# The experts' outputs added to the tokens two blocks at a time, the last squares summed on VectorE

## Chip, cores and metric

The kernel runs on one core of a Trainium2 chip. The metric is the device time of one execution in microseconds, the median of several runs.

## What is computed

A conformer convolution block with a feed-forward layer, then a second block: projections, a short convolution and a spatial gating unit, a mixture of 16 experts, and a last RMS norm. T = 256 tokens, D = 2048 features. Only the experts and the last norm matter here:

```python
def hierarchical_moe(x, w_rg, b_rg, w_re, b_re, w_gate, w_up, w_down):
    ...
    gate = ((pg * oh_g)[:, :, None] * w_inner[:, None, :]).reshape(-1, N_EXPERTS)
    hid = jax.nn.silu(jnp.einsum('td,edf->tef', t, w_gate)) * jnp.einsum('td,edf->tef', t, w_up)
    y = jnp.einsum('tef,efd->td', hid * gate[:, :, None], w_down)
    return y.reshape(bsz, s, d)

    ...
    h = h + hierarchical_moe(rms_norm_2(h, norm_ffn_g[l]), ...)
    return rms_norm_2(h, norm_final_g)
```

## The kernel before

Features lie on the 128 partitions: the tokens `h` are 16 blocks (KB) of 128 features by 256 tokens in float32. Weights are float32 in memory; each 128x1024 half of a weight tile is loaded by SyncE into one of 8 raw buffers, ScalarE makes a high part of it (`hi`, L75) and VectorE the rest (`lo`, L83). A raw buffer is loaded anew when its low part is done. TensorE multiplies by both parts, with separate records for loading the stationary operand (PEld) and for the product (PE).

In the experts' stage (`experts`, from about 1700 us) at most 64 tokens of each expert are gathered. For expert e, `into(e)` multiplies 16 halves of the gate and up weights into banks 0 and 1, `between(e)` makes the hidden values out of them (L1167 to L1200: copies out, two folds on TensorE, silu, product, high and low part), and `down(e)` multiplies 8 halves of the down weights; every two of these fill a bank, and ScalarE copies it to `Yt` (L1215). The turns run in 0, in 1, out 0, in 2, out 1 and so on. In the last turns (`out 13`, `out 14`, `in 15`) only the last expert's are different: out 13 and out 14 follow each other, and `out 15` ends the stage.

An expert's output is then put back at its tokens, a **scatter**: for block k a product of `Yt` with the placement matrix `scat[e]` into a bank of a ring of six, for two experts in one bank (the first and the last expert go alone), and an add of the bank to `h` by VectorE (L1152). The scatters wait in the list `todo`. After each half `fill` adds a credit of 0.5 us (0.3 in `into(15)`, 1 in `down(15)`, at most 1 in all) and takes scatters while the credit is above zero, each at 0.43 us times its experts. What has to follow on VectorE and ScalarE is put into `posts`, and `beat`, at the start of each half, writes all posts and then the next high and low parts. The stream is written ahead: at a half, the low part of the half two places later follows.

The order on each engine is the order in which the program writes it, and an engine that waits holds what is behind it. In the last expert's scatters an add is followed by a square on ScalarE (L1158, into `sq` with two buffers, into `acc` for blocks 0 and 8, into `lone` for the last three), and GpSimd adds the squares to `acc` (L535). `natural_sums` sums `acc` and the `lone`s on TensorE; the norm's factor and the 16 output blocks (L1278) follow.

Of the kernel before, what the change touches and what calls it, by code (L numbers as in the profile page):

```python
# [7 lines left out]
F32 = mybir.dt.float32  # L8
# [3 lines left out]
ACT = mybir.ActivationFunctionType  # L12
# [3 lines left out]
P = 128  # L16
D = 2048
KB = D // P
T = 256
# [111 lines left out]
def network(ctx, tc, a, out):  # L131
# [946 lines left out]
    def experts(hot, stream, extra):  # L1078
# [64 lines left out]
            scat[e], rsl[e] = sc, rs  # L1143

        def scatter(k, es):
            b, o = spare()
            for n, e in enumerate(es):
                mm(o[:, :T], Yt[e % 3][:, k * P : (k + 1) * P], scat[e], n == 0, n == len(es) - 1)
                left[e] -= 1

            def add():
                nc.vector.tensor_tensor(h[:, k, :], h[:, k, :], o[:, :T], OP.add)  # L1152
                if NE - 1 in es:
                    post(square)

            def square():
                sq = square_to(k)
                nc.scalar.activation(sq, h[:, k, :], ACT.Square)  # L1158
                post(lambda: add_square(sq, k, True))

            post(add, b)

# [39 lines left out]
        def down(e):  # L1202
            while e >= 3 and left[e - 3] > 0:
                todo.popleft()[1]()
            hd = hids.pop(e)
            left[e] = KB
            for c in range(4):
                b, o = taken()
                for n in range(2):
                    hi, lo = beat()  # L1210
                    for f in range(2):
                        product(o, hd[:, 2 * n + f, :], hi, lo, f, n == 0 and f == 0, n == 1 and f == 1)
                    if n == 1:
                        def out_of_bank(c=c, b=b, o=o):
                            nc.scalar.copy(Yt[e % 3][:, c * 512 : (c + 1) * 512], o)  # L1215
                            ring.append(b)

                            es = (e,) if e in (0, NE - 1) else (e - 1, e)
                            if e == NE - 1 or e % 2 == 0:
                                for k in range(4 * c, 4 * c + 4):  # L1220
                                    todo.append((0.43 * len(es), lambda k=k: scatter(k, es)))
                        post(out_of_bank)
                    fill(FILL_DOWN if e < NE - 1 else 1)

# [46 lines left out]
                posts.popleft()()  # L1271


        natural_sums(bank[2], 2, lone)
        rsqrt(rp, bank[2][:, :4:2], eps6)
        to_all(rp, bank[3][:, :T])
        for k in range(KB):
# [72 lines left out]
```

## Time and profile before

| what | value |
|---|---|
| median of 3 runs | 2271.34 us (2270.51 to 2272.91) |
| the profiled execution's own time | 2271.37 us |
| its span | 2269.6 us |
| PE busy, share of the span | 2217.8 us, 98% |
| PEld busy | 2077.4 us, 92% |
| DVE busy | 1597.0 us, 70% |
| ACT busy | 1256.9 us, 55% |
| POOL busy | 215.7 us, 10% |
| mean over the span, read and written | 224 GB/s |

PE is TensorE's products, PEld its loads of the stationary operand, DVE VectorE, ACT ScalarE, POOL GpSimd. Products are pipelined and their ends are modelled, so PE's 98% says little about how much room is left; where TensorE waits shows in the weight loads, whose rows carry the idle time ahead of them and what ended it. The stages differ, so shares are to be read by stage: the experts' stage lies between 1700 and 2254 us.

### The profile page before, as it was taken

What the parts mean: (1) busy time and instruction counts of PE and PEld (TensorE: products, weight loads), DVE (VectorE), ACT (ScalarE), POOL (GpSimd) and SP (SyncE); (2) the same over time, 40 slices, a digit from 0 to 9 for tenths busy, and PEclk for the clock granted to TensorE, in tenths of its full rate; (3) what the DMA queues carried; (4) which work ended last, traced back from release to release, by engine and by line L of the source; (5) the groups of instructions that cost most, each with busy time, mean ns of one, the idle gap of its engine ahead of it and who ended that gap; (6) DMA issues with size and microseconds to landing.
All of it is one profiled execution on the core that took longest, in us unless ns stands there. A gap on an engine that the chain in (4) does not pass through costs nothing. (4 is left out here: it accounts for less than half of the span.)

```text
span 2269.6 us, 41689 instructions
## 1 busy us (share of the span) xinstructions
PE 2217.8 (98%) x16539; PEld 2077.4 (92%) x16539; DVE 1597.0 (70%) x2259; ACT 1256.9 (55%) x1638; POOL 215.7 (10%) x162
## 2 busy tenths in 40 slices
PE   6999999999999999999999999999999999999996
PEld 6999899999999999999899999999977878778775
DVE  6999767655544455555875665566569899998996
ACT  4446554544434444444553444444578988878774
POOL 5798200000000000000100000000000000000001
PEclk8999999999999999999999999999999999999998
DMA  6554355565665566656656556656559999999993
GB/s 217 164 170 164 103 195 168 189 195 194 193 197 195 186 199 193 194 187 197 216 179 203 190 188 191 195 185 204 181 174 363 362 376 353 333 368 327 385 345 151
DMA packets 139964, 508.90 MB, mean 224 GB/s; under 512 B 15552, under 2 KB 15568, under 8 KB 139760
## 3 DMA queue, kind: packets, MB, share of 16 engines
q1 hardware_dynamic: 139104, 503.88, 65.2%
q8 instruction: 131, 2.15, 0.4%
q0 software_dynamic: 656, 2.27, 0.3%
q14 instruction: 73, 0.60, 0.1%
HBM read 503.99 MB, written 2.10 MB: 223 GB/s over the span
## 5 line engine op out<-in xcount | busy, mean ns | idle before, releaser
L83 DVE TENSOR_TENSOR lo<-raw,hi 128x1024 fp32r<-128x1024 f32 x884 | 1063.6, 1222 | 531.6 <-PE bank L164 468.0
L75 ACT CAST hi<-raw 128x1024 fp32r<-128x1024 f32 x952 | 987.0, 1054 | 738.9 <-PE bank L164 566.1
L164 PE MATMUL bank<-aH,hi 128*128 128x256 f32 (+1 forms) x3456 | 966.4, 280 | 6.3 <-ACT aH L243 4.7
L164 PE MATMUL bank<-aL,hi 128*128 128x256 f32 (+1 forms) x3456 | 960.2, 279 | 8.3 <-DVE aL L245 8.3
L164 PE MATMUL bank<-aH,lo 128*128 128x256 f32 (+1 forms) x3456 | 963.4, 279 | 0.0
L164 PEld LDWEIGHTS bank<-aH,hi 128*128 128x128 f32 x3456 | 653.2, 189 | 9.1 <-ACT aH L243 5.1
L164 PEld LDWEIGHTS bank<-aL,hi 128*128 128x128 f32 x3456 | 649.6, 189 | 9.8 <-DVE aL L245 9.5
L164 PEld LDWEIGHTS bank<-aH,lo 128*128 128x128 f32 x3456 | 653.0, 189 | 0.0
L535 POOL TENSOR_TENSOR acc<-acc,sq 128x256 f32<-128x256 f32 x23 | 18.5, 805 | 1913.8 <-ACT sq L676 723.4
L164 PE MATMUL bank<-hidH,lo 128*128 128x256 f32 x704 | 194.3, 276 | 0.0
L164 PE MATMUL bank<-hidH,hi 128*128 128x256 f32 x704 | 194.3, 276 | 0.0
L164 PE MATMUL bank<-hidL,hi 128*128 128x256 f32 x704 | 194.3, 276 | 0.0
L83 POOL TENSOR_TENSOR lo<-raw,hi 128x1024 fp32r<-128x1024 f32 x68 | 163.4, 2417 | 52.2 <-ACT hi L75 32.3
L284 DVE SCALAR_TENSOR_TENSOR bank<-glu,vec,bank 128x256 f32<-128x256 f32 x387 | 160.7, 482 | 1.9
L164 PEld LDWEIGHTS bank<-hidH,hi 128*128 128x128 f32 x704 | 132.2, 188 | 0.0
L164 PEld LDWEIGHTS bank<-hidL,hi 128*128 128x128 f32 x704 | 132.2, 188 | 0.0
L164 PEld LDWEIGHTS bank<-hidH,lo 128*128 128x128 f32 x704 | 132.2, 188 | 0.0
L164 PE MATMUL bank<-hi,aH 128*128 128x512 f32 x320 | 128.4, 418 | 0.8 <-ACT gu_first L1167 0.6
L164 PE MATMUL bank<-hi,aL 128*128 128x512 f32 x320 | 126.1, 410 | 0.0
L164 PE MATMUL bank<-lo,aH 128*128 128x512 f32 x320 | 122.8, 400 | 0.8 <-DVE lo L83 0.8
L164 PE MATMUL bank<-hi,hd_first 128*128 128x512 f32 x256 | 109.9, 429 | 0.7 <-DVE hd_first L1200 0.5
L164 PE MATMUL bank<-lo,aL 128*128 128x512 f32 x256 | 103.4, 404 | 0.6 <-DVE lo L83 0.6
(284 smaller groups left out, 2177.7 us busy)
## 6 DMA issues: line engine op xcount, KB each, us to landing
raw<-egu SPq DMA_DIRECT2D x256, 512.0 KB, 5.9
raw<-gu SPq DMA_DIRECT2D x176, 512.0 KB, 4.3
raw<-w SPq DMA_DIRECT2D x144, 512.0 KB, 4.3
raw<-edn SPq DMA_DIRECT2D x128, 512.0 KB, 6.1
raw<-dn SPq DMA_DIRECT2D x88, 512.0 KB, 4.3
raw<-cw_in SPq DMA_DIRECT2D x64, 512.0 KB, 3.6
raw<-cw_out SPq DMA_DIRECT2D x32, 512.0 KB, 3.9
raw<-wup SPq DMA_DIRECT2D x32, 512.0 KB, 4.5
```

Of the source, the lines that this page charges most:

```text
L75: self.nc.scalar.copy(hi, self.source(self.n_high))
L83: eng.tensor_tensor(lo, self.source(self.n_low), self.highs[self.n_low].bitcast(F32), OP.subtract)
L164: nc.tensor.matmul(o, l, r, start=start, stop=stop, skip_group_check=True)
L284: nc.vector.scalar_tensor_tensor(dw[:, j, :] if t == end - 1 else ta, gl, V("w_dw", j * TAPS + t), early[j % 2] if t == 1 else ta, OP.mult ...
L535: (nc.gpsimd if n or gpsimd else nc.vector).tensor_tensor(acc[:, n, :], acc[:, n, :], sq, OP.add)
```

## The change

`scatter(k, es)` now takes blocks k and k + 1: two products per expert into the two halves of one bank, and one add of 128x2x256 by VectorE. It is put on the list for every second block at twice the price, 0.86 us times its experts. In the last expert's scatters ScalarE squares both blocks in one instruction (into `acc` for blocks 0 and 1, into a buffer `sq2` of which there is one for the others, into two `lone`s for the last two), and VectorE, not GpSimd, adds the squares to the whole of `acc`. `natural_sums` takes two `lone`s instead of three.

```diff
--- before.py
+++ after.py
@@ -1143,20 +1143,31 @@
             scat[e], rsl[e] = sc, rs
 
         def scatter(k, es):
+
             b, o = spare()
-            for n, e in enumerate(es):
-                mm(o[:, :T], Yt[e % 3][:, k * P : (k + 1) * P], scat[e], n == 0, n == len(es) - 1)
-                left[e] -= 1
+            for i in range(2):
+                for n, e in enumerate(es):
+                    mm(o[:, i * T : (i + 1) * T], Yt[e % 3][:, (k + i) * P : (k + i + 1) * P], scat[e], i == 0 and n == 0, n == len(es) - 1)
+            for e in es:
+                left[e] -= 2
+            two = h[:, k : k + 2, :]
 
             def add():
-                nc.vector.tensor_tensor(h[:, k, :], h[:, k, :], o[:, :T], OP.add)
+                nc.vector.tensor_tensor(two, two, o.rearrange("p (i t) -> p i t", i=2), OP.add)
                 if NE - 1 in es:
                     post(square)
 
             def square():
-                sq = square_to(k)
-                nc.scalar.activation(sq, h[:, k, :], ACT.Square)
-                post(lambda: add_square(sq, k, True))
+                if k >= KB - 2:
+                    nc.scalar.activation(lone[0], two[:, 0], ACT.Square)
+                    nc.scalar.activation(lone[1], two[:, 1], ACT.Square)
+                    return
+                if k == 0:
+                    nc.scalar.activation(acc, two, ACT.Square)
+                    return
+                sq = tmp.tile([P, 2, T], F32, tag="sq2", bufs=1, name=f"last{k}_{turn_of[0]}")
+                nc.scalar.activation(sq, two, ACT.Square)
+                post(lambda: nc.vector.tensor_tensor(acc, acc, sq, OP.add))
 
             post(add, b)
 
@@ -1217,8 +1228,8 @@
 
                             es = (e,) if e in (0, NE - 1) else (e - 1, e)
                             if e == NE - 1 or e % 2 == 0:
-                                for k in range(4 * c, 4 * c + 4):
-                                    todo.append((0.43 * len(es), lambda k=k: scatter(k, es)))
+                                for k in (4 * c, 4 * c + 2):
+                                    todo.append((0.86 * len(es), lambda k=k: scatter(k, es)))
                         post(out_of_bank)
                     fill(FILL_DOWN if e < NE - 1 else 1)
 
@@ -1271,7 +1282,7 @@
                 posts.popleft()()
 
 
-        natural_sums(bank[2], 2, lone)
+        natural_sums(bank[2], 2, lone[:2])
         rsqrt(rp, bank[2][:, :4:2], eps6)
         to_all(rp, bank[3][:, :T])
         for k in range(KB):
```

What moves in the order is shown at three places. The first is VectorE, where down halves (654, 655) of expert 2 have just ended and gate/up halves of expert 4 begin; `lo656` is the low part of half 656, `x0` holds the tokens `h`, and an add of `x0` and a bank belongs to a scatter. Before:

```order
L83 TENSOR_TENSOR lo656_20448<-raw656_20333,hi656_20434 128x1024
L1152 TENSOR_TENSOR x0_83<-x0_83,bank4_64 128x256
L83 TENSOR_TENSOR lo657_20462<-raw657_20348,hi657_20446 128x1024
L1152 TENSOR_TENSOR x0_83<-x0_83,bank5_65 128x256
L1200 TENSOR_TENSOR hd3_first_20360<-sg3_first_20359,hd3_first_20360 128x4x64
L83 TENSOR_TENSOR lo658_20477<-raw658_20368,hi658_20460 128x1024
L83 TENSOR_TENSOR lo659_20487<-raw659_20378,hi659_20475 128x1024
L1152 TENSOR_TENSOR x0_83<-x0_83,bank7_67 128x256
L83 TENSOR_TENSOR lo660_20500<-raw660_20389,hi660_20485 128x1024
L83 TENSOR_TENSOR lo661_20510<-raw661_20409,hi661_20498 128x1024
L1152 TENSOR_TENSOR x0_83<-x0_83,bank2_62 128x256
L83 TENSOR_TENSOR lo662_20523<-raw662_20424,hi662_20508 128x1024
```

With the change:

```order
L83 TENSOR_TENSOR lo656_20441<-raw656_20325,hi656_20427 128x1024
L83 TENSOR_TENSOR lo657_20452<-raw657_20340,hi657_20439 128x1024
L1156 TENSOR_TENSOR x0_83<-x0_83,bank2_62 128x2x256
L1211 TENSOR_TENSOR hd3_first_20352<-sg3_first_20351,hd3_first_20352 128x4x64
L83 TENSOR_TENSOR lo658_20469<-raw658_20360,hi658_20450 128x1024
L83 TENSOR_TENSOR lo659_20479<-raw659_20370,hi659_20467 128x1024
L83 TENSOR_TENSOR lo660_20489<-raw660_20381,hi660_20477 128x1024
L83 TENSOR_TENSOR lo661_20499<-raw661_20400,hi661_20487 128x1024
L1156 TENSOR_TENSOR x0_83<-x0_83,bank7_67 128x2x256
L83 TENSOR_TENSOR lo662_20514<-raw662_20415,hi662_20497 128x1024
L83 TENSOR_TENSOR lo663_20524<-raw663_20431,hi663_20512 128x1024
L83 TENSOR_TENSOR lo664_20534<-raw664_20443,hi664_20522 128x1024
```

Each add now stands for two blocks, and four low parts (three at the next) follow each other between two adds; one low part of half n + 3 still follows the add of the scatter that TensorE does after half n, and `hd3` (L1200, now L1211) stands between the two.

The second is TensorE at the same place; `sc1` and `sc2` are the placement matrices of experts 1 and 2, `aH` the gathered tokens. Before:

```order
L164 MATMUL bank5_65<-sc1_first_19686,y_120 128x256
L164 MATMUL bank5_65<-sc2_first_19985,yx_19251 128x256
L164 MATMUL bank0_60<-hi656_20434,aH_118 128x512
L164 MATMUL bank0_60<-lo656_20448,aH_118 128x512
L164 MATMUL bank1_61<-hi656_20434,aH_118 128x512
L164 MATMUL bank1_61<-lo656_20448,aH_118 128x512
L164 MATMUL bank0_60<-hi657_20446,aH_118 128x512
L164 MATMUL bank0_60<-lo657_20462,aH_118 128x512
L164 MATMUL bank1_61<-hi657_20446,aH_118 128x512
L164 MATMUL bank1_61<-lo657_20462,aH_118 128x512
L164 MATMUL bank7_67<-sc1_first_19686,y_120 128x256
L164 MATMUL bank7_67<-sc2_first_19985,yx_19251 128x256
```

With the change:

```order
L164 MATMUL bank2_62<-sc1_first_19686,y_120 128x256
L164 MATMUL bank2_62<-sc2_first_19977,yx_19251 128x256
L164 MATMUL bank2_62<-sc1_first_19686,y_120 128x256
L164 MATMUL bank2_62<-sc2_first_19977,yx_19251 128x256
L164 MATMUL bank0_60<-hi656_20427,aH_118 128x512
L164 MATMUL bank0_60<-lo656_20441,aH_118 128x512
L164 MATMUL bank1_61<-hi656_20427,aH_118 128x512
L164 MATMUL bank1_61<-lo656_20441,aH_118 128x512
L164 MATMUL bank0_60<-hi657_20439,aH_118 128x512
L164 MATMUL bank0_60<-lo657_20452,aH_118 128x512
L164 MATMUL bank1_61<-hi657_20439,aH_118 128x512
L164 MATMUL bank1_61<-lo657_20452,aH_118 128x512
```

Four products of scatters stand in a row instead of two, and the next four follow only behind half 659, where before two follow behind half 657.

The third is ScalarE in the last expert, from its first square on; `y` is the copy of a finished bank to `Yt`. Before:

```order
L1158 ACTIVATE acc_121<-x0_83 128x256
L1158 ACTIVATE sq_48_24208<-x0_83 128x256
L1158 ACTIVATE sq_49_24210<-x0_83 128x256
L1215 COPY y_120<-bank3_63 128x512
L1158 ACTIVATE sq_50_24225<-x0_83 128x256
L1158 ACTIVATE sq_51_24236<-x0_83 128x256
L1158 ACTIVATE sq_52_24238<-x0_83 128x256
L1158 ACTIVATE sq_53_24240<-x0_83 128x256
L1215 COPY y_120<-bank7_67 128x512
```

With the change:

```order
L1166 ACTIVATE acc_121<-x0_83 128x512
L1169 ACTIVATE last2_first_24143<-x0_83 128x512
L1226 COPY y_120<-bank0_60 128x512
L1169 ACTIVATE last4_first_24163<-x0_83 128x512
L1169 ACTIVATE last6_first_24165<-x0_83 128x512
L1226 COPY y_120<-bank7_67 128x512
L1169 ACTIVATE last8_first_24184<-x0_83 128x512
L1169 ACTIVATE last10_first_24186<-x0_83 128x512
L1226 COPY y_120<-bank4_64 128x512
```

Between two copies of a bank stand two squares of 128x512 instead of three or four of 128x256, and each square but the first goes to the one buffer `last`.

## Rows read from the trace of the kernel before

**Rows 1.** Windows: busy us (instructions) of each engine, clock granted, DMA share, GB/s.
```profile
core 0: us, PE busy (x) PEld busy (x) DVE busy (x) ACT busy (x) POOL busy (x), PEclk, DMA share, GB/s
1700.00:2250.00 550.00, 539.48 (x2490) 426.49 (x2491) 501.66 (x591) 447.95 (x553) 8.55 (x10) 1.00 0.93 345
...
1862.00:1907.00 45.00, 45.00 (x215) 37.72 (x215) 41.02 (x52) 33.78 (x42) 0.00 (x0) 1.00 0.96 351
2000.00:2010.00 10.00, 8.90 (x45) 6.75 (x45) 7.98 (x9) 8.23 (x12) 0.00 (x0) 1.00 1.03 421
```

**Rows 2.** Instructions by line and form, 1690 to 2260 us, VectorE.
```profile
L83 DVE TENSOR_TENSOR lo<-raw,hi 128x1024 fp32r<-128x1024 f32 x373 | 441.8, 1220 | 19.7 <-ACT hi L75 18.1 <-PE bank L164 0.5 <-issue 0.3
...
L1152 DVE TENSOR_TENSOR x<-x,bank 128x256 f32<-128x256 f32 x144 | 59.1, 418 | 26.1 <-PE bank L164 24.6
...
L1200 DVE TENSOR_TENSOR hd_first<-sg_first,hd_first 128x256 fp32r<-128x256 f32 x16 | 6.7, 418 | 0.0
```

**Rows 3.** Timeline, 1880 to 1896 us, a scatter stretch: start, duration, engine, line, operation.
```profile
1881.59 0.19 PEld L164 LDWEIGHTS bank<-hi,aH 128*128 128x128 f32 x1
...
1884.28 0.19 PEld L164 LDWEIGHTS bank<-hi,aL 128*128 128x128 f32 x1
...
1884.50 0.19 PEld L164 LDWEIGHTS bank<-lo,aL 128*128 128x128 f32 x1
1884.70 0.42 DVE L1152 TENSOR_TENSOR x<-x,bank 128x256 f32<-128x256 f32 x1
...
1885.04 2.35 DVE L83 TENSOR_TENSOR lo<-raw,hi 128x1024 fp32r<-128x1024 f32 x2
...
1886.97 0.19 PEld L164 LDWEIGHTS bank<-hi,aL 128*128 128x128 f32 x1
...
1888.75 0.19 PEld L164 LDWEIGHTS bank<-hi,aL 128*128 128x128 f32 x1
```

**Rows 4.** Waits of the weight loads: 1862.5 to 1907 us, then 1838.6 to 1861.
```profile
PEld bank L164 <- issue: 0.7, 2, 0.4
...
PEld bank L164 <- DVE lo L83: 6.3, 16, 0.7
```

**Rows 5.** Timeline of a scatter-free stretch: VectorE, then weight loads.
```profile
1839.21 16.05 DVE L83 TENSOR_TENSOR lo<-raw,hi 128x1024 fp32r<-128x1024 f32 x14
...
1842.83 0.19 PEld L164 LDWEIGHTS bank<-lo,aH 128*128 128x128 f32 x1 [0.37 <-DVE lo L83]
...
1843.96 0.19 PEld L164 LDWEIGHTS bank<-lo,aH 128*128 128x128 f32 x1 [0.37 <-DVE lo L83]
```

**Rows 6.** Instructions by line and form, whole span: 128x512 on VectorE, squares on ACT.
```profile
L547 DVE TENSOR_TENSOR acc<-acc,sqb 128x512 f32<-128x512 f32 x14 | 9.7, 692 | 3.9 <-ACT sqb L545 3.9
...
L846 DVE TENSOR_TENSOR vm<-bank,bsb 128x512 f32<-128x512 f32 x4 | 2.8, 690 | 2.8 <-PE bank L164 2.7
...
L545 ACT ACTIVATE sqb<-x 128x512 f32<-128x512 f32 x14 | 8.7, 624 | 0.0
```

**Rows 7.** Timeline, 2213 to 2222 us, gate/up halves of the last expert.
```profile
2213.59 0.41 DVE L1152 TENSOR_TENSOR x<-x,bank 128x256 f32<-128x256 f32 x1
...
2213.92 3.49 DVE L83 TENSOR_TENSOR lo<-raw,hi 128x1024 fp32r<-128x1024 f32 x3
...
2214.78 0.19 PEld L164 LDWEIGHTS bank<-hi,aL 128*128 128x128 f32 x1
...
2215.19 0.19 PEld L164 LDWEIGHTS bank<-lo,aL 128*128 128x128 f32 x1 [0.22 <-DVE lo L83]
...
2215.30 0.19 PEld L164 LDWEIGHTS bank<-hi,aL 128*128 128x128 f32 x1
```

**Rows 8.** Timeline, 2240 to 2271 us, the end: ACT and weight loads.
```profile
2243.03 0.42 ACT L1158 ACTIVATE sq<-x 128x256 f32<-128x256 f32 x1 [1.27 <-POOL acc L535]
...
2245.60 1.16 PEld L164 LDWEIGHTS bank<-sc_first,y 128*128 128x128 f32 x6 [1.57 <-ACT y L1215]
...
2248.13 0.59 ACT L1215 COPY y<-bank 128x512 f32<-128x512 f32 x1
...
2248.77 1.59 PEld L164 LDWEIGHTS bank<-sc_first,y 128*128 128x128 f32 x8 [0.65 <-ACT y L1215]
```

## The prediction

> **What bounds the kernel now.** I read the stage first, since the change touches only the experts' stage, from about 1700 us to the end. Over 1700 to 2250 us the clock granted to TensorE is 1.00; weight loads (PEld) are busy 426 of 550 us, VectorE 502, the DMA engines 0.93 of the time [rows 1]. Three engines near their limit do not say which one is last, so the second view was the waits of the weight loads, stretch by stretch. The stage alternates. In **scatter stretches** (1862 to 1907 us is one) the experts' outputs are added to the tokens between the weight halves, and there the weight loads wait for nothing but 0.7 us of issue: TensorE alone is the bound, and VectorE's idle time costs nothing. In **scatter-free stretches** (1838.6 to 1861 us) they wait 16 times for VectorE's low parts, 6.3 us [rows 4], and VectorE runs 14 low parts without a gap, 1.14 us from start to start, which the wait of 0.37 us in each half shows on TensorE's side [rows 5]. In those stretches stands not one of the adds that the change touches.
>
> So the adds lie where VectorE is not last, and the third view is the timeline of one scatter stretch, to see how far it is from being last [rows 3]. From one first weight load after a scatter to the next: 2.69 us with two halves, 1.78 us with one, hence 0.91 us a half and 0.87 us a scatter of two experts. VectorE's add starts 0.42 us after the first load behind its scatter (1884.28 to 1884.70), occupies 0.34 us until the next start, then two low parts follow without a gap until the next add: the two engines are just level, with VectorE served in order.
>
> **The change part by part.** *Adds.* 144 adds of 256 columns (418 ns [rows 2]) become 72 of 512. The new form, bank and SBUF in, 128x512 out, has its nearest rows at 690 and 692 ns [rows 6]. Instructions overlap by 0.08 us (0.42 long, 0.34 apart), so an add goes from 0.34 to 0.61 us from start to start, and a pair of blocks from 0.68 to 0.61: VectorE gains 72 x 0.07 = 5.0 us, by durations 72 x (0.836 - 0.690) = 10.5 us. All but the ends of it lie in scatter stretches where no weight load waits [rows 4]: I take 0 of it.
>
> *What moves.* The credit (0.5 us a half) lets a scatter of 0.86 pass every one or two halves; one of 1.72 passes every three or four. TensorE's own work is the same, 1.72 us a double scatter. But the order of VectorE shows the add always behind the low part of the second half after its scatter and ahead of that of the third, before and after. Count from the first load after a scatter. Before: add at 0.42, low part of the third half done at 0.42 + 0.34 + 1.22 = 1.98, usable 0.05 later (2213.92 + 1.22 to 2215.19 [rows 7]), at 2.03; TensorE asks for it at 0.22 + 2 x 0.91 = 2.04, or at 2.91 where a scatter stands ahead of it, as it mostly does. Nothing is lost, which is what [rows 4] shows. Now: 0.42 + 0.61 + 1.22 + 0.05 = 2.30, and with three or four halves no scatter stands ahead: 0.26 late. Part is hidden, since the load after a late one follows at 0.11 instead of 0.23 us (2215.19 to 2215.30 [rows 7]): lost 0.14. For a fourth half the lag grows by 1.14 - 0.91 = 0.23, all lost.
>
> Who waits: the low parts are queued behind the add on VectorE, and TensorE waits for them. For each pair of experts (the order repeats this six times) there are six runs of three or four halves: six third halves at 0.14 in an expert's gate/up halves and about 0.10 in the one run of down halves (0.80 together), three fourth halves (0.66), and once the step L1200 (418 ns [rows 2], 0.34 from start to start) stands between the add and the low part of a third half (0.34). Sum 1.80 us a pair, 6 x 1.80 = **10.8 us**. Bounds: 0.06 a third half, as the one late load at 2215.19 lost (due at 2214.78 + 0.23 = 2215.01, 0.18 late, 0.12 hidden [rows 7]), gives 1.30 a pair; 0.20, were less hidden, 2.2: 7.8 to 13.4 us.
>
> *The last pair and the last expert.* At credit 0.3 the double scatter comes every six halves, twice, and after three once: 0.14 + 2 x (0.14 + 3 x 0.23) = 1.8. Before, with three halves to an add, VectorE already paced this place and the late loads lost some 0.2 [rows 7]: **+1.6 us**, between 0.8 and 2.0.
>
> *The first expert.* Its scatters are single and short; eight pairs of adds at 0.07 less are -0.6 at most, if VectorE paces them: **-0.4 us**, between -0.6 and 0.
>
> *The end.* GpSimd's eleven adds of squares go; six adds of 512 columns come to VectorE, 692 ns each, and ACT squares two blocks at once, 624 ns by the nearest row [rows 6] against 0.42. One third `lone` goes, four short matmul records. Before, ACT waited for GpSimd (1.27 us at 2243.03) and so moved the experts' banks late: the scatters at 2245.60 and 2248.77 waited 1.57 and 0.65 us for it [rows 8]. Now ACT's squares have one buffer, freed by VectorE's add, which stands behind the adds of the next two pairs of blocks; two squares stand ahead of each bank copy. Followed step by step with these durations, the second and third copies come within 0.3 us of where they were, the last, behind the square of blocks 10 and 11, at 2249.7 instead of 2248.13 [rows 8], with the final scatters behind it: **+1.4 us**. Bounds: -1.0, if nothing but GpSimd's wait goes, to +2.5, if each of four copies waits for one more square.
>
> Sum: 10.8 + 1.6 - 0.4 + 1.4 = +13.4 us. The profiled execution took 2271.37 us (span 2269.6), the median of three runs is 2271.34, so one carries over to the other. **Forecast 2284.8 us**; bounds added up, +7.0 to +17.9: 2278 to 2289.
>
> **The rivals.** *VectorE's relief pays.* If VectorE is the bound also where it looks level, the gain on it is a gain of the stage: -5.0 to -10.5 us, 2261 to 2266. For it: 91% busy over the stage. Against it: no wait for it in the scatter stretches, where all the saved time lies [rows 4]. It decides if low parts were late behind the shorter adds. The Trainium skill (Perfetto Trace Analysis, Identifying the Most-Contended Engine) says to improve first the engine with the highest occupancy, TensorE being judged by its weight-load share; by that rule VectorE (91% against 78%) is the one, and the relief counts. The waits by stretch speak against it for this change, and I give this case 0.12.
>
> *The weights' transfers set the pace.* Then TensorE's short stalls are made up before the next weights arrive, and only the end counts, -1.0 to +2.5: 2270 to 2274, about 2272. For it: 1.03 of the DMA's time and 421 GB/s at 2000 to 2010 us. Against it: in the scatter stretch it moves 351 GB/s with no load waiting, well under 421 [rows 1, 4]. The Trainium skill (Perfetto Trace Analysis, Engine Utilization) puts a core's full memory rate at 358 GB/s; by it the stage's 345 would be nearly all there is. The 421 GB/s of the trace show more, so I leave this case, together with stalls that turn out half as long or hidden, at 0.16.
>
> *The change does not shorten the list of adds.* The order shows 72 and not 144, so nothing is left for this.
>
> **How the numbers follow.** Forecast case 0.72, within 2278 to 2289; transfers or hidden stalls 0.16; relief 0.12. The range leaves out the relief and the outermost of the forecast: 2269 to 2289. A measurement of this kernel tells some 0.2%, 4.5 us, from no change. Faster 0.12, same 0.16, slower 0.72.
>
> **What would show it.** In the profile of the changed kernel: waits of the weight loads for L83 inside the scatter stretches, about 0.3 us idle (0.26 late and the usual 0.04) in third halves, 0.4 in fourth ones, some nine a pair; the stretch from 1862 on longer by about 1.8 us a pair, the scatter-free stretches as long as before; VectorE's busy time down by about 10 us and its idle time up by more than that; an add near 690 ns. The forecast is wrong if scatter stretches still show no wait for L83, if the low part of the third half comes ahead of the add, or if the scatter-free stretches shorten.

## The result, and the profile after

The changed kernel takes **2286.51 us** (median of 4 runs, 2284.97 to 2287.99) beside 2272.12 us for the kernel before (median of 4): ratio **1.0058**, 95% interval 1.0043 to 1.0073, that is 10 to 17 us slower. The forecast was 2284.8 us. The profiled execution of after took 2286.72 us (span 2285.0), so the two profiled executions differ by 15.4 us. Not all of this is the change. The first placement product of the experts' stage starts at 1696.42 us in the profile of before, in those of the twelve other kernels and after between 1695.75 and 1701.96, and nothing ahead of it was changed. So from here on the **stage** counts: from that product to the weight load of `rp`, behind the last sums. Rows of weight loads, before:

```profile
1696.42 0.72 PEld L164 LDWEIGHTS bank<-placeT,idt 32*128 32x128 f32 x4 [0.36 <-issue]
...
2253.86 0.52 PEld L164 LDWEIGHTS bank<-idt,rp 128*128 128x128 f32 x4 [0.64 <-DVE rp L206]
```

The same of after (start, duration, engine, line, operation, and the idle time ahead with what ended it):

```profile
1699.39 0.72 PEld L164 LDWEIGHTS bank<-placeT,idt 32*128 32x128 f32 x4 [0.36 <-issue]
...
2268.70 0.93 PEld L164 LDWEIGHTS bank<-idt,rp 128*128 128x128 f32 x4 [0.64 <-DVE rp L206]
```

557.44 us became 569.31: the change costs **11.9 us** in the stage, 3.0 us of the profiles' difference lies ahead of it and 0.5 behind. 11.9 is inside the interval of the timed runs. A stage is read from one profiled execution. Parts of it in which several kernels have the very same instructions tell how far that goes: from the first placement product to the last, after and the runs pairs_only and end_own_buffers below took 536.6, 537.2 and 537.3 us. So a difference of under a microsecond between two stages is not told from chance.

What VectorE does by line and form, after, 1690 to 2275 us (us in all, mean ns, idle ahead), answers [rows 2]:

```profile
L83 DVE TENSOR_TENSOR lo<-raw,hi 128x1024 fp32r<-128x1024 f32 x374 | 438.8, 1220 | 17.2 <-ACT hi L75 15.6 <-PE bank L164 0.7 <-issue 0.3
L1156 DVE TENSOR_TENSOR x<-x,bank 128x512 f32<-128x512 f32 x72 | 49.1, 686 | 44.1 <-PE bank L164 44.0
...
L1170 DVE TENSOR_TENSOR acc<-acc,last_first 128x512 f32<-128x512 f32 x6 | 4.1, 688 | 1.5 <-ACT last_first L1169 1.5
```

The adds cost VectorE 10.0 us less (49.1 against 59.1), as meant. Its whole busy time fell by only 3.6 us (1597.0 to 1593.4), not by the 10 that the prediction named: six adds of squares came (4.1 us), and two instructions without a gap between them overlap, which durations count twice. VectorE's idle time ahead of adds went from 26.1 to 44.1 us: it was not given less to wait for, but more. Who waits now shows in the waits of the weight loads, 1700 to 2290 us (us in total, times, longest), before and then after:

```profile
PEld bank L164 <- DVE lo L83: 27.7, 70, 1.0
...
PEld bank L164 <- ACT y L1215: 8.2, 9, 1.6
```

```profile
PEld bank L164 <- DVE lo L83: 48.5, 132, 1.0
...
PEld bank L164 <- ACT y L1226: 8.8, 8, 2.0
...
PEld bank L164 <- DVE acc L1170: 1.8, 1, 1.8
```

62 more waits for low parts and 20.8 us more of them. (Each wait holds the usual gap of 0.04 us between two loads, and the load behind it comes 0.12 us sooner than usual, so the loss is less than the sum.) They stand where they were expected: the stretch of [rows 3 and 4], which waited for nothing but issue, now reads (1865 to 1911 us)

```profile
PEld bank L164 <- DVE lo L83: 3.0, 9, 0.6
...
PEld bank L164 <- issue: 0.7, 2, 0.4
```

and one late low part in the timeline, which answers [rows 3], looks so:

```profile
1883.07 0.19 PEld L164 LDWEIGHTS bank<-hi,aH 128*128 128x128 f32 x1
...
1883.48 0.69 DVE L1156 TENSOR_TENSOR x<-x,bank 128x512 f32<-128x512 f32 x1 [0.52 <-PE bank L164]
...
1884.09 3.49 DVE L83 TENSOR_TENSOR lo<-raw,hi 128x1024 fp32r<-128x1024 f32 x3
...
1884.89 0.19 PEld L164 LDWEIGHTS bank<-hi,aH 128*128 128x128 f32 x1
1885.36 0.19 PEld L164 LDWEIGHTS bank<-lo,aH 128*128 128x128 f32 x1 [0.28 <-DVE lo L83]
1885.47 0.19 PEld L164 LDWEIGHTS bank<-hi,aH 128*128 128x128 f32 x1
```

The first load behind a double scatter is at 1883.07. The add starts 0.41 us later, VectorE comes to the third half's low part after another 0.61, and TensorE gets it at 1885.36, 2.29 us after the first load; it was due at 1884.89 + 0.23 = 1885.12. So it came 0.24 us late, and the next load followed at 0.11 instead of 0.23. The end answers [rows 8]:

```profile
2249.12 1.59 PEld L164 LDWEIGHTS bank<-sc_first,y 128*128 128x128 f32 x8 [0.62 <-ACT y L1226]
...
2258.31 1.59 PEld L164 LDWEIGHTS bank<-sc_first,y 128*128 128x128 f32 x8 [1.49 <-ACT y L1226]
...
2262.83 1.59 PEld L164 LDWEIGHTS bank<-sc_first,y 128*128 128x128 f32 x8 [2.03 <-ACT y L1226]
...
2266.20 0.97 PEld L164 LDWEIGHTS bank<-ones,acc 128*128 128x128 f32 x8 [1.78 <-DVE acc L1170]
```

The last scatters wait 2.03 us for their bank copy (0.65 before [rows 8]), and the sums wait 1.78 us for VectorE's last add of squares, where before they waited 0.34 us for GpSimd:

```profile
2251.36 0.52 PEld L164 LDWEIGHTS bank<-ones,acc 128*128 128x128 f32 x4 [0.34 <-POOLq L1288]
```

### The profile page after: what moved, and what is told of

The parts are those of the page before. It is cut to its first block, busy times and chain, and to the rows that moved or that the text cites. A ratio compares the mean times of both kernels' runs of the same rounds, so it can differ in the third digit from the quotient of the medians.

```text
span 2285.0 us, 41620 instructions
## 1 busy us (share of the span) xinstructions
PE 2231.1 (98%) x16535; PEld 2075.0 (91%) x16535; DVE 1593.4 (70%) x2193; ACT 1253.8 (55%) x1631; POOL 206.3 (9%) x151
## 4 chain that ended last, share of the span: by engine, by line
PE 91%; DVE 3%; ACT 3%; issue 1%; DMA 1%; DVEq 0%; ACTq 0%
PE bank L164 90%; ACT hi L75 2%; DVE lo L83 1%; DMA raw<-edn 1%; DVE bank L394 1%; DVE u L241 0%; DMA raw<-egu 0%; DVE aL L245 0%; DVE y L1289 0%; PE bank L167 0%; ACT aL L1027 0%; ACT aH L1027 0%; ACT gu_first L1178 0%; DVE x L1156 0%; ACT y L1226 0%
## 5 line engine op out<-in xcount | busy, mean ns | idle before, releaser
L83 DVE TENSOR_TENSOR lo<-raw,hi 128x1024 fp32r<-128x1024 f32 x884 | 1059.3, 1222 | 530.6 <-PE bank L164 469.9
L83 POOL TENSOR_TENSOR lo<-raw,hi 128x1024 fp32r<-128x1024 f32 x68 | 163.5, 2419 | 51.8 <-ACT hi L75 32.3
L535 POOL TENSOR_TENSOR acc<-acc,sq 128x256 f32<-128x256 f32 x12 | 8.9, 740 | 1335.2 <-ACT sq L676 723.4
```

Of the source, the lines that this page charges most:

```text
L83: eng.tensor_tensor(lo, self.source(self.n_low), self.highs[self.n_low].bitcast(F32), OP.subtract)
L535: (nc.gpsimd if n or gpsimd else nc.vector).tensor_tensor(acc[:, n, :], acc[:, n, :], sq, OP.add)
```

## The experiments

Theory **Q** (queue): the loss comes from the low parts that stand behind a longer add in VectorE's order, in stretches where no scatter gives VectorE time to catch up; the end costs a little. Rivals: **B** (bursts), four scatter products in a row are worse in any form, whatever VectorE's add; **E** (end), the loss lies in the last expert; **T** (transfers), part of the loss is given back because the weights set the pace elsewhere. Each run gives its ratio to the kernel before, timed beside it, and the stage of one profiled execution. The ratio is estimated from the single runs of both kernels and need not be the quotient of the two medians. All stages and times:

| kernel | stage, us | against before | median, us | ratio (95%) |
|---|---|---|---|---|
| before | 557.44 | | 2272.12 | |
| after | 569.31 | +11.87 | 2286.51 | 1.0058 (1.0043 to 1.0073) |
| pairs_only | 567.53 | +10.09 | 2283.70 | 1.0045 (1.0030 to 1.0059) |
| add_one_beat_later | 559.61 | +2.17 | 2275.91 | 1.0012 (1.0002 to 1.0022) |
| bursts_narrow_adds | 560.38 | +2.94 | 2276.51 | 1.0014 (1.0003 to 1.0025) |
| streams_one_further | 561.27 | +3.83 | 2276.82 | 1.0015 (1.0006 to 1.0025) |
| later_adds_old_end | 556.99 | -0.45 | 2272.03 | 0.9998 (0.9990 to 1.0007) |
| end_own_buffers | 568.62 | +11.18 | 2283.78 | 1.0052 (1.0038 to 1.0067) |
| best_of_both | 556.06 | -1.38 | 2271.49 | 0.9997 (0.9989 to 1.0006) |
| scatters_spread | 552.82 | -4.62 | 2267.36 | 0.9979 (0.9969 to 0.9989) |
| spread_old_scatters | 552.33 | -5.11 | 2267.39 | 0.9987 (0.9978 to 0.9995) |
| spread_and_end | 552.45 | -4.99 | 2268.75 | 0.9984 (0.9975 to 0.9993) |
| light_before | 554.06 | -3.38 | 2269.49 | 0.9979 (0.9967 to 0.9992) |
| light_after | 568.42 | +10.98 | 2284.14 | 1.0043 (1.0023 to 1.0063) |

(The kernels were timed in groups, each beside the kernel before: it took 2273.32 us in the group of the first four experiments, 2272.17 in that of later_adds_old_end, end_own_buffers, best_of_both and scatters_spread, 2271.23 in that of the two spread kernels and 2274.14 in that of the light ones.)

### pairs_only: the changed scatters, the old end

After, but the last expert's scatters, adds, squares and sums as before:

```diff
-                                for k in (4 * c, 4 * c + 2):
-                                    todo.append((0.86 * len(es), lambda k=k: scatter(k, es)))
+                                if e == NE - 1:
+                                    for k in range(4 * c, 4 * c + 4):
+                                        todo.append((0.43 * len(es), lambda k=k: scatter_last(k, es)))
+                                else:
+                                    for k in (4 * c, 4 * c + 2):
+                                        todo.append((0.86 * len(es), lambda k=k: scatter(k, es)))
```

> Double scatters for all experts but the last; the last expert's scatters, squares and GpSimd's sums as in the kernel before. Theory (the low part of the third half is queued behind the wide add): nine late low parts for each of the six pairs stay, 0.24 to 0.60 us of idle weight loads each, so some 12 us over before, about 2284. Rival (the end, with VectorE's squares, is what costs): at most 3 us over before, about 2275, and no late low parts.

The stage is 10.1 us longer than before, with 132 waits for low parts, as many as in after. So the pairs of experts carry most of the 11.9 us. The new end costs 1.8 us by the two stages, and 2.4 if only what follows the last placement product is compared (32.75 us in after, 30.31 here), where the two kernels differ. E falls as the main cause.

### add_one_beat_later: the same adds, one place later

After, with the double adds of all experts but the last written one beat later, behind one more low part:

```diff
+            posts.append(lambda: posts.append(once))
+            reads[b] = once
...
-            post(add, b)
+            (post if NE - 1 in es else post_late)(add, b)
```

> The kernel after, but the wide add of every scatter (last expert excepted) is written one half later, so that the low part of the third half stands ahead of it on VectorE. TensorE's order is unchanged, four products of scatters in a row. Theory (queue order on VectorE): the fourth half's low part is done at 0.42 + 0.61 + 1.22 + 0.05 = 2.30 us and wanted at 2.95, so the waits in the scatter stretches go, about 10 us back: some 2 to 4 us over before, about 2275. Rival (TensorE's longer bursts of scatters cost by themselves): the time of the kernel after stays, about 2286.

The same instructions, in another order on VectorE, and all but 2.2 of the 11.9 us are gone. In the weight loads, 1700 to 2290 us:

```profile
PEld bank L164 <- DVE lo L83: 26.9, 67, 1.0
```

67 waits, where before had 70 and after 132; the scatter stretches have none. This is the run that settles Q: the price is neither the wide add nor the burst as such but the place of the add behind the burst. The timed runs agree, 1.0012 in place of 1.0058. What is left, 2.2 us, is the end.

### bursts_narrow_adds: the bursts without the wide add

Before, with two single scatters at once at double price, each with its own add of 256 columns:

```diff
-                                for k in range(4 * c, 4 * c + 4):
-                                    todo.append((0.43 * len(es), lambda k=k: scatter(k, es)))
+                                for k in range(4 * c, 4 * c + 4, 1 if e == NE - 1 else 2):
+                                    both = (k,) if e == NE - 1 else (k, k + 1)
+                                    todo.append((0.43 * len(both) * len(es), lambda both=both: [scatter(k, es) for k in both]))
```

> The kernel before, but its single scatters are taken two at a time (last expert excepted): TensorE's bursts are those of the change, the adds are two of 256 columns from two banks. Theory (what counts is when VectorE gets free behind the burst): the first add runs during the burst, the second at 0.42, so the third low part comes at 0.42 + 0.34 + 1.22 + 0.05 = 2.03, in time; the fourth at 3.17 against 2.95, 0.10 lost; with the hidden step between, 0.21 and 0.23 once. 0.64 us a pair, 3.9 for six, about 1.2 for the last pair: some 5 us over before, 2277. Rival (the burst itself): 11 us or more, 2283.

+2.9 us, where some 5 were expected. The waits of one pair are the four that theory Q puts there:

```profile
1810.85 0.19 PEld L164 LDWEIGHTS bank<-lo,aH 128*128 128x128 f32 x1 [0.34 <-DVE lo L83]
1811.99 0.19 PEld L164 LDWEIGHTS bank<-lo,aH 128*128 128x128 f32 x1 [0.36 <-DVE lo L83]
...
1821.95 0.19 PEld L164 LDWEIGHTS bank<-lo,aL 128*128 128x128 f32 x1 [0.22 <-DVE lo L83]
...
1833.16 0.19 PEld L164 LDWEIGHTS bank<-lo,hd_first 128*128 128x128 f32 x1 [0.21 <-DVE lo L83]
```

So the burst alone does cost, but through the same queue, and it is under a third of what the bursts cost with the wide add (2.9 against 10.1 us). Rival B holds for no more than that; together with the run ahead, it is not a cause of its own. The count was right and the net too high; no run tells for this kernel why.

### streams_one_further: high and low parts written one half further ahead

After with `MOE_HI, MOE_LO = 5, 4`:

```diff
-MOE_HI, MOE_LO = 4, 3
+MOE_HI, MOE_LO = 5, 4
```

> The kernel after with the high and low parts written one half further ahead (5 and 4 instead of 4 and 3), adds unchanged. The low part of the third half then stands ahead of the add by another way. Theory: waits in the scatter stretches go as with the later add, some 2 to 4 us over before, about 2275, unless the steps of the hidden values, which now also come one low part later, hold TensorE at the last experts (up to 2 us more). Rival (bursts): 2286 stays.

The waits for low parts fall below even those of before, but the stage stays 3.8 us longer:

```profile
PEld bank L164 <- DVE lo L83: 19.6, 48, 1.0
PEld bank L164 <- ACT y L1226: 13.0, 9, 2.0
...
PEld bank L164 <- DVE hot_first L1013: 3.9, 3, 1.8
PEld bank L164 <- ACT yx L1226: 3.7, 3, 1.6
```

The remedy moves the wait to the bank copies on ScalarE (13.0 instead of 8.8 us and 3.7 instead of 2.3) and to VectorE's one-hots (3.9 instead of 2.6), which now have one more high or low part written ahead of them. (That this is what holds them is read from the order; no run tests it alone.)

### later_adds_old_end: late adds and the old end

pairs_only with the adds of add_one_beat_later.

```diff
-            post(lambda: nc.vector.tensor_tensor(two, two, o.rearrange("p (i t) -> p i t", i=2), OP.add), b)
+            post_late(lambda: nc.vector.tensor_tensor(two, two, o.rearrange("p (i t) -> p i t", i=2), OP.add), b)
```

> Double scatters with wide adds written one half later for all experts but the last; the last expert as in the kernel before. From the first placement product to the norm's factor the runs took 557.4 us before, 559.6 with later adds and the new end; there the end alone took 31.3 and 33.8 us, with one block less to scatter (0.87 us). Theory: without the new end about 1 us under before in this stretch, 2272, same as before. Rival (wide adds still cost something in the scatter stretches): 2 us over before or more.

0.45 us less than before by one profile, ratio 0.9998 (-2.3 to +1.6 us by its interval): with the loss in the queue gone, the whole relief of VectorE is worth less than can be measured. This is the direct test of the rival that VectorE's relief pays.

### end_own_buffers: the squares' one buffer

After, with the last squares in `yx` instead of the one `sq2`; `yx` holds outputs of experts up to 14 and is free by then:

```diff
-                sq = tmp.tile([P, 2, T], F32, tag="sq2", bufs=1, name=f"last{k}_{turn_of[0]}")
+                sq = yx[:, k % 8 : k % 8 + 2, :]
```

> The kernel after, with a buffer of its own for each of the last expert's squares up to four (in yx, which is free by then) instead of one. Theory (ACT's squares wait for VectorE's sums through the one buffer, and the bank copies behind them are late): 0.7 to 1.5 us back at the end, 2285. Rival (the squares wait for the adds anyway, or the end is set by VectorE's work): the end stays within 0.3 us.

0.7 us back in the stage. Ahead of the last placement product the two kernels have the same instructions; behind it, where they differ, after took 32.75 us and this kernel 31.35, so 1.4 us came back at the end, the upper part of the 0.7 to 1.5 expected, and the rest of the two stages' difference is chance. The last two waits for bank copies, 1.49 and 2.03 us in after, shrink, that for the sums does not:

```profile
2256.40 1.59 PEld L164 LDWEIGHTS bank<-sc_first,y 128*128 128x128 f32 x8 [0.64 <-ACT y L1226]
2260.37 1.59 PEld L164 LDWEIGHTS bank<-sc_first,y 128*128 128x128 f32 x8 [1.49 <-ACT y L1226]
2263.75 0.97 PEld L164 LDWEIGHTS bank<-ones,acc 128*128 128x128 f32 x8 [1.78 <-DVE acc L1170]
```

So the single buffer is the larger part of the end's cost, 1.4 of some 2.4 us. The rest, 1.0 us against pairs_only, is left in the chain of scatter, add, square and add of squares, which now runs through VectorE for two blocks at once; no run takes that chain apart further.

### best_of_both: late adds, own buffers, bank copies ahead of the squares

add_one_beat_later with the buffers of end_own_buffers, and the last expert's bank copies at the head of the posts:

```diff
-                        post(out_of_bank)
+                        (posts.appendleft if e == NE - 1 else post)(out_of_bank)
```

> The kernel after with later adds, a buffer of its own for the squares, and the last expert's bank copies written ahead of the squares on ACT. Theory (at the end the squares ahead of the copies hold the last scatters; waits of 0.63, 1.85, 1.50 and 2.02 us): 2 to 4 us of the end go, so some 1 us under before, 2271. Rival (the end is VectorE's work): like add_one_beat_later, 2276.

The stage is 1.4 us shorter than before, 0.9 shorter than later_adds_old_end (0.7 behind the last placement product alone), though the sums now wait 2.5 us for `acc`; the timed ratio, 0.9997, does not tell it from before. GpSimd can be left out of the end without loss, and with hardly any gain.

### scatters_spread: scatters into the stretches that have none

later_adds_old_end with the credit of a half lowered to 0.33 in nine turns, so that scatters last into the scatter-free stretches:

```diff
-                    fill(FILL_DOWN if e < NE - 1 else 1)
+                    fill((0.33 if e in (3, 7, 11) else FILL_DOWN) if e < NE - 1 else 1)
...
-                    fill(FILL_LAST if e == NE - 1 else FILL_GU if nxt is None else FILL_GATHER)
+                    fill(FILL_LAST if e == NE - 1 else (0.33 if e in (4, 5, 8, 9, 12, 13) else FILL_GU) if nxt is None else FILL_GATHER)
```

> As later_adds_old_end, and where a pair's last gate/up stretch holds no gathers (pairs 1, 3 and 5) the credit is 0.33 us a half instead of 0.5, so that the scatters reach into the stretch that VectorE paces. TensorE's idle time there (0.22 us a half) would take them up: by VectorE's and TensorE's durations 1.25 us a half against a mean of 1.30 now, about 2 us for each of three pairs. Theory A (the two engines set the pace): 4 to 6 us under later_adds_old_end. Theory B (the weights' transfers, 421 GB/s at best, 1.25 us a half, hold the stretch already): 0 to 2 us under it.

The stage is 552.82 us, 4.2 less than without the spread, as theory A had it, and the kernel takes 0.2% less than before (0.9979). TensorE's work is the same; more of it is done where TensorE waited for low parts (26.7 us of such waits in later_adds_old_end):

```profile
PEld bank L164 <- DVE lo L83: 22.6, 62, 1.0
```

### spread_old_scatters and spread_and_end: what the spread needs

The same two lines on the kernel before, and on best_of_both.

> The kernel before with one edit: the share of a scatter queue that is worked off after each half is 0.33 in place of 0.5 in two scatter stretches out of six experts' (the first product of experts 4, 5, 8, 9, 12, 13 and the second of 3, 7, 11), with the old single scatters, adds and end. In the run scatters_spread the same edit, on top of wide adds written one beat later, took 4.2 us from the stage (from the first placement product to the load of rp 552.82 against 556.99 us). Theory A, the spread pays by itself, because the stretches without scatters wait for the weights' transfers and scatter products fill those waits: the stage is about 553.3 us (557.4 less 4.2), the time about 2268, ratio 0.998. Theory B, it pays only with wide late adds, since more stretches then hold an add in front of a low part: no more than 1 us off, 2271 to 2273, ratio 0.9995 to 1.0005. Waits of weight loads for the low part by A fall from 27.7 us to about 24 us.

> Both halves that gained, in one kernel: wide adds one beat later, the share 0.33 in those stretches, the last expert's pairs with their squares in the unused buffers of the token blocks and the last bank copies written ahead of the squares. Stage by sums: 552.8 (scatters_spread) less 0.9 (best_of_both 556.06 against later_adds_old_end 556.99) = 551.9 us, time 2266.4, ratio 0.9975 (0.9965 to 0.9985). If the two interfere (the last pair's scatters start from another backlog, so that the end finds a longer queue), the stage is no shorter than 552.8 us and the time 2267 to 2269.

The spread pays by itself: 552.33 us with the old single scatters, 5.1 less than before, the waits for low parts down to 24.2 us, as theory A had them, and those for bank copies from 11.2 to 8.8 us. Its reason is not borne out in all: ScalarE waits as long for raw loads as before (20.9 against 20.1 us); what the scatters fill are TensorE's waits for the low parts and copies. On best_of_both it gives 552.45 where the sum of the parts gave 551.9, a difference within chance. So the three kernels with the spread are level, and **the wide adds bring nothing to it**. The simplest does as well as any of those tried: the kernel before with other credits at two places.

### light_before and light_after: a quarter of the transfers left out

The forecast's own numbers left one thing open: in the profile the six pairs cost less than their waits. These two runs leave out every fourth transfer of the experts' weights, with all engines' work kept, in before and in after:

```diff
+            if self.loaded >= 2 * len(self.order) - 384 and self.loaded % 4 == 3:
+                t = self.last
+            else:
                 t = self.raw.tile([P, 1024], F32, tag="raw", name=f"raw{self.loaded}")
                 self.nc.sync.dma_start(out=t, in_=self.order[i][0][:, s * 1024 : (s + 1) * 1024])
+            self.last = t
```

> The kernel before with a quarter fewer transfers in the experts' stage: every fourth half of the experts' weights is not loaded, its high and low parts are made from the raw buffer of the half ahead of it (so a quarter of the experts' weights is replaced by their neighbours; the work of ScalarE, VectorE and TensorE is the same). It is the base for light_after: what counts is the stage from the first placement product to the load of rp (557.4 us before, 569.3 after, +11.9). Waits of ScalarE for raw loads in 1700 to 2250 us fall from 20.1 us to under 5. If transfers pace the scatter-free stretches, the stage is 2 to 5 us shorter than 557.4; if VectorE's queue alone does, it is within 1 us of it.

> The changed kernel with the same quarter of the transfers left out (same replacement of a quarter of the experts' weights). Theory T: of the six pairs' late low parts (1.73 us a pair, 10.4 us) some 1.9 us was given back because the stretches without scatters wait for transfers, which get ahead while TensorE is late. With light transfers nothing is left to give back: light_after less light_before is 13 to 14.5 us in the stage. Rival V: the give-back comes from the waits for ScalarE's bank copies and the order on VectorE, whatever the transfers: the difference stays at 11.4 to 12.4 us.

ScalarE's waits for raw loads are gone from the list of both. The stages are 554.06 and 568.42 us: **14.4 us apart, where with all transfers it is 11.9**. Theory T said 13 to 14.5, its rival at most 12.4. Lighter transfers give before 3.4 us and after only 0.9.

Where this lies is to be seen where the scatters of a pair begin. There TensorE waits for ScalarE's copy of a bank. The first, third and fifth pair begin with such a wait of 1.4 us in every one of these kernels, the light ones too. The second, fourth and sixth differ; before, the fourth:

```profile
2004.95 0.30 PEld L164 LDWEIGHTS bank<-sc_first,yx 128*128 128x128 f32 x2 [1.19 <-ACT yx L1215]
```

The second and sixth wait 0.94 and 0.58 us. In after the waits at these three places are 0.65, 0.48 and 0 us, here the fourth pair again:

```profile
2011.48 0.30 PEld L164 LDWEIGHTS bank<-sc_first,yx 128*128 128x128 f32 x2 [0.48 <-ACT yx L1226]
```

With light transfers none of the three is left in either kernel. The reading that fits is that late transfers make ScalarE's high parts late, and the bank copy in the same queue with them. ScalarE's own waits for raw loads around the fourth pair (1996 to 2034 us before, 2004 to 2041 after) are, before:

```profile
ACT hi L75 <- DMA raw<-egu: 3.1, 7, 1.0
```

and after:

```profile
ACT hi L75 <- DMA raw<-egu: 0.4, 1, 0.4
```

The transfers run at the same rate in both there (windows: busy us of PE, PEld, DVE, ACT, POOL, then clock, DMA share, GB/s), before and after:

```profile
1996.00:2008.00 12.00, 10.90 (x47) 7.51 (x47) 10.64 (x13) 9.37 (x11) 0.00 (x0) 1.00 1.03 420
```

```profile
2004.00:2016.00 12.00, 11.88 (x56) 8.61 (x55) 11.19 (x13) 9.80 (x13) 0.00 (x0) 1.00 1.03 420
```

That they had got ahead in after, while TensorE was late, fits this, but its size is not settled. Of the 2.5 us between 11.9 and 14.4, 1.6 lie in the six pairs and 0.4 in the first expert; 0.5 lie in the last sums, where no weights come in (the loads for `lone` took 1.47 us in light_after and 0.97 in after). pairs_only and end_own_buffers, with the same pairs as after, have 2.0 and 1.8 us of these three waits, nearer to before's 2.7 than to after's 1.1. And the timed medians do not show it: 14.65 us between the two light kernels, 14.39 with all transfers.

## Why the prediction was right, point by point

The sum by its own terms. The stage is cut at its first placement product, at the first scatter of a pair and at the last placement product; a term is after less before between its two cuts, from one profile of each kernel:

| term | forecast, us | measured | with light transfers |
|---|---|---|---|
| first expert | -0.4 | -0.3 | +0.1 |
| six pairs | +10.8 (7.8 to 13.4) | +8.5 | +10.1 |
| last pair, in the last expert | +1.6 (0.8 to 2.0) | +1.4 | +1.4 |
| the end | +1.4 (-1.0 to +2.5) | +2.3 | +2.8 |
| stage | +13.4 | +11.9 | +14.4 |

(The last pair and the end are parted at a placement product ahead of which after has scattered one block more; 0.87 us, the price of a scatter by [rows 3], is moved from the one to the other. In the forecast's own working three fourth halves at 0.23 are 0.69 us and not 0.66, and the bounds of the pairs come to 8.2 and 13.2 us with the losses that are named; neither moves a number by more than 0.4 us.)

**The mechanism held.** Where the load was to wait and by how much came out as worked out. A pair has nine waits for L83, as said; those of experts 1 and 2 are

```profile
1809.20 0.19 PEld L164 LDWEIGHTS bank<-lo,aH 128*128 128x128 f32 x1 [0.60 <-DVE lo L83]
1810.34 0.19 PEld L164 LDWEIGHTS bank<-lo,aH 128*128 128x128 f32 x1 [0.37 <-DVE lo L83]
1814.95 0.19 PEld L164 LDWEIGHTS bank<-lo,aH 128*128 128x128 f32 x1 [0.28 <-DVE lo L83]
1819.56 0.19 PEld L164 LDWEIGHTS bank<-lo,aL 128*128 128x128 f32 x1 [0.27 <-DVE lo L83]
1820.70 0.19 PEld L164 LDWEIGHTS bank<-lo,aL 128*128 128x128 f32 x1 [0.37 <-DVE lo L83]
1825.31 0.19 PEld L164 LDWEIGHTS bank<-lo,aL 128*128 128x128 f32 x1 [0.28 <-DVE lo L83]
1831.17 0.19 PEld L164 LDWEIGHTS bank<-lo,hd_first 128*128 128x128 f32 x1 [0.27 <-DVE lo L83]
1832.31 0.19 PEld L164 LDWEIGHTS bank<-lo,hd_first 128*128 128x128 f32 x1 [0.37 <-DVE lo L83]
```

and one of 0.24 at 1804.27: third halves 0.24 to 0.28, fourth 0.37, and 0.60 where the hidden step stands between. With light transfers, where these waits stand almost alone, the pairs are 1.5 to 1.8 us longer each, 10.1 in all; 1.80 and 10.8 were forecast.

**The six pairs were over-sized**, 10.8 for 8.5, and the step that failed is the tacit one that before's own waits in a scatter stretch stay as they are, so that what the stretch loses behind the adds is lost for good. The prediction read its stretch from 1862.5 us on, where nothing but issue is waited for [rows 4]. The scatters of that pair begin at 1860.16, and ahead of the window lies a wait for a bank copy:

```profile
1861.52 1.16 PEld L164 LDWEIGHTS bank<-sc_first,y 128*128 128x128 f32 x6 [0.94 <-ACT y L1215]
```

Of the 2.3 us, 0.7 is size (10.1 with light transfers). The other 1.6 are such waits, 2.7 us in before and 1.1 in after.

The rival of the weights' transfers was given 0.16 as an alternative; it is true in part, beside the forecast and not in place of it, as far as single profiles tell (pairs_only and end_own_buffers put the six pairs at +9.0 and +8.8). It is not the scatter-free stretches that gave it back: from the last scatter of a pair to the first of the next, after less before is the same with all transfers as with the light ones, within 0.2 us, in five of the six; in the one ahead of the fourth pair it is 0.4 us less. The rival's weighing, 351 GB/s in the scatter stretch against 421 [rows 1, 4], went by the middle of a scatter stretch; at the start of the fourth pair the transfers run at 420 GB/s, and there the time is lost. The Trainium skill (Perfetto Trace Analysis, Engine Utilization), which was cited for its 358 GB/s, says in a note to that figure that a core alone in its pair can draw up to some 435 GB/s, the limit of its 16 DMA engines. The trace agrees: 420 over 12 us in both kernels.

**The end was under-sized**, 1.4 for 2.3 (2.4 by pairs_only), within its bounds. The step that failed is what follows the last bank copy: the steps were followed up to the copies, and the sums were taken to wait as before. The last copy does come late (2.03 us of wait instead of 0.65), but then the sums wait 1.78 us for VectorE's last add of squares instead of 0.34 for GpSimd. In all, the last expert's scatters wait 5.0 us for bank copies in after and 3.1 in before: the waits for GpSimd [rows 8], which looked like the cost of the old end, were replaced by longer ones for VectorE.

**The last pair** came out as sized. **The first expert** did so by luck: the term is -0.3 in after, but -0.1 and +0.1 in pairs_only and end_own_buffers, which have the same instructions there, and +0.1 with light transfers. What differs is a wait for a bank copy at its first scatter (0.79 us before, 0.37 after, 0.57 and 0.77 in those two). That VectorE's adds pace it, the condition of the term, is not shown.

**The relief of VectorE** was not worth the 5.0 to 10.5 us of the rival: 0.45 us in one profile and -0.14 in the medians (later_adds_old_end), not told from nothing. The rule of the Trainium skill (Perfetto Trace Analysis, Identifying the Most-Contended Engine), to improve first the engine with the highest occupancy, misleads here when VectorE's 91% of the whole stage is read by it: its adds took 10.0 us less and the kernel became slower, and with the order mended it stayed the same.

**The total** fits better than its terms, and that is luck in part. The errors of the pairs (-2.3) and of the end (+0.9) partly cancel, and the stages differ by 11.9 us where 13.4 was forecast. That the medians differ by 14.4 (interval 10 to 17) does not tell 13.4 from 11.9: both lie within the interval. The terms are tested by the stage, not by the last digit of the median.

**What stays open.** How much of the pairs' loss the transfers give back needs more than one profile of each kernel. Why spread_and_end timed a little above the other two spread kernels though the stages are level is not settled; the intervals of the three overlap. Whether other credits than 0.33 do better was not tried.

## What to carry to other kernels

Two operations merged into one are cheaper by their own time and dearer by their place: on an engine that is served in order, ask what is queued behind the longer one, and whether what gave it slack has moved away. When an engine's instructions must grow, write them one place later in its order before giving up the change; here that was worth 10 us. And in a stage whose stretches have different limits, moving work from the full stretches to the waiting ones can pay more than making that work cheaper: here 5.1 us against 0.45. Such a stage is also to be read from the first instruction of a stretch on, since a wait at its start is easily left outside the window.

## What was not expected of the hardware

- The add of 128x512 with a bank as an operand took 686 ns, about as the nearest rows said (690 and 692 [rows 6]), but followed at 0.61 us by the next instruction; so 0.08 us of each VectorE instruction lies beside the next at 256 and at 512 columns alike.
- With a granted clock of 0.988 to 0.990 over the span in every profile, the same instructions ahead of the stage ended up to 6 us apart (1695.75 to 1701.96 us). One profile of each kernel can't be compared over the whole span to better than that.
- Leaving out a quarter of the transfers, at the same work of all engines, gave 3.4 us of a stage of 557 whose DMA engines were 0.93 busy; their share fell to 0.77.
